# One activation table set for Ln and Exp, a reordered first norm, two tiles per block of h, and early weights in a two-layer hybrid decoder

## The chip, the cores and the metric

The kernel runs on one core of one Trainium2 chip. The metric is device time in microseconds (us), the median of several executions. All arithmetic is in 32-bit floats. Large products are made of three TensorE products of halves ("hi" and "lo" parts in the fp32r type), so that a product of two fp32 tiles costs three matmuls.

## The reference

Two layers, each an RMS norm, one input projection, three causal mixers that read the same normalised input, SiLU gates, one output projection and a residual add; one RMS norm after the last layer. The sequence is 1024 long, the model 1024 wide.

```python
def hybrid_layer(x, ...):
    h = rmsnorm(x, norm_gain)
    proj = h @ w_in
    (gq, gk, gv, gb, ga, gz, mq, mkv, mkr, mz, lx, lz) = jnp.split(proj, offsets, axis=-1)
    ...
    o_a = gated_delta_rule(q, k, v, g, beta)          # 4 heads of 128, chunks of 64
    o_a = rmsnorm(o_a, gdn_out_norm).reshape(B, S, GDN_WIDTH).astype(dt) * jax.nn.silu(gz)
    ...
    o_b = causal_block_attention(qf, kf, vm) * jax.nn.silu(mz)   # 8 heads, latent q and kv
    ...
    o_c = rg_lru(u, ...) * jax.nn.silu(lz)            # 512 channels, scan over the sequence
    mixed = jnp.concatenate([o_a, o_b, o_c], axis=-1)
    return x + mixed @ w_out

def rmsnorm(x, gain):
    y = x * lax.rsqrt(jnp.mean(x * x, axis=-1, keepdims=True) + RMS_EPS)
    return y * gain
```

## The kernel before

Activations lie transposed: 128 channels on the partitions, the 1024 positions along the free axis, in two halves of 512 (`n` = 0, 1). The normalised input `h` is eight blocks of 128 channels, each as a hi tile (`self.hh[k]`) and a lo tile (`self.hl[k]`). An output tile of the input projection is 128 channels; there are 38 of them per layer (`w_in`), each 2 halves x 8 blocks x 3 matmuls = 48 matmuls of 512 columns into one PSUM tile `pbig` of two banks. Two `pbig` tiles exist at a time.

**The order of the work** is a planner's. The program is traced in Python order, each instruction with a priority that grows with the trace; `self.prio(-LOW)` makes an instruction urgent, `self.prio(LOW)` makes it filler. The planner lays the instructions out on each engine by a model of their durations, and each engine then runs its own list strictly in order, waiting on semaphores. The load of an activation table is put in by a pass that comes after: ahead of an activation whose function isn't in the set that is loaded, it loads the first set that has it. Exp, Tanh, Square and Copy are in the set loaded first; Ln is in another. DMAs are all issued by SP's queue, also in order.

A layer has two stages. `phase_a` makes the input projection and runs the GDN and LRU mixers (`gates`, `gdn_tok`, `gdn_pre`, `gdn_inverse`, `gdn_prep`, `gdn_scan`, `gdn_norm`, `lat_q`, `lat_kv`, `lru`), with input-projection tiles as filler between the parts of the GDN chain. `phase_c` makes the latent attention, one head after the other, its softmax with Exp, and adds the output projection in pieces (`out_proj`, `out_proj_last`).

**The weights** of a projection tile are loaded by `load_w` (line 97): a DMA into `wst`, a cast to `whi` on VectorE (on ScalarE for narrow ones), and the remainder `wlo` on GpSimd. The pool `pw` has two of each, so a third tile's `whi` and `wlo` can be made only after the first tile's products have been done.

**The norm.** `rms_bcast` (line 180) adds up squares over the channels with matmuls against ones, then r = exp(-0.5 ln(mean + eps)) on ScalarE: an Ln, then an Exp. Line 186 is an Ln of one column that brings the table load ahead of the real Ln. `norm_half` (line 201) makes h block by block: `hf` = x * gain * r on VectorE, the hi cast on ScalarE, the lo remainder on VectorE, or with `share` on GpSimd for every other block. `first_norm` (line 924) does this for both halves of the input in turn; at the end of layer 0 it is done from `out_proj_last` (line 848), at the end of layer 1 the final norm writes the output.

**The first two tiles.** `gates` calls `in_tile(l, MT_MISC, MT_K)`: both tiles of a half are traced one after the other, MISC over all eight blocks of h, then K over all eight. The gates' inputs are copied out of MISC (line 219) and transposed (line 224).

**Memory.** Pools are laid out on a stack in the order of the `with` lines of `build` (line 878). `pw` of the next layer (2 x (wst + whi + wlo) of 4 KB per partition, 24 KB) starts where phase_c's first pool starts. That is `pp` (line 917): the softmax tiles P, four of 2 KB and four of 4 KB, 24 KB, in which `out_proj_last` also keeps its weights `wl`. After it lie `px` (four xt tiles, 8 KB), `pw` of phase_c (12 KB), and `pc` with the tiles k (eight of 2 KB), q, qr, v, o and others. A tile that is put where another was waits for that one's readers.

Of the kernel before, what the change touches and what calls it, by code (L numbers as in the profile page):

```python
# [16 lines left out]
DM = 1024  # L17
L = 2
H2 = 512
# [44 lines left out]
class Trunk:  # L64
# [20 lines left out]
    def act(self, out, in_, func, **kw):  # L85
        self.nc.scalar.activation(out, in_, func, **kw)  # L86
# [10 lines left out]
    def load_w(self, src, nk, cols, eng=None, pool=None):  # L97
# [6 lines left out]
        nc.sync.dma_start(st[:, :n], src.rearrange("p k c -> p (k c)"))  # L104
        hi = pool.tile([128, wn], F32R, name="whi", tag="whi")
        lo = pool.tile([128, wn], F32R, name="wlo", tag="wlo")
        with self.prio(-self.LOW):
            if wn <= 512:
                nc.scalar.copy(hi[:, :n], st[:, :n])  # L109
            else:  # L110
                nc.vector.tensor_copy(hi[:, :n], st[:, :n])  # L111
            (eng or nc.gpsimd).tensor_tensor(lo[:, :n], st[:, :n], hi[:, :n].bitcast(F32), ALU.subtract)  # L112
# [3 lines left out]
    def mm3(self, out, pairs):  # L116

        nc = self.nc
        n = len(pairs)
        for j, (ah, al, bh, bl) in enumerate(pairs):  # L120
            nc.tensor.matmul(out, ah, bh, start=(j == 0), stop=False)  # L121
            nc.tensor.matmul(out, ah, bl, start=False, stop=False)  # L122
            nc.tensor.matmul(out, al, bh, start=False, stop=(j == n - 1))  # L123
# [7 lines left out]
    def in_tile(self, l, *ms):  # L131

        if ms[0] not in self.ready:
            tiles = []
            for m in ms:
                hi, lo = self.early.pop(m, None) or self.load_w(self.i["w_in"][l, m], 8, 128)
                self.ready[m] = self.big()
                tiles.append((hi, lo, self.ready[m]))
            with self.prio(self.LOW):
                for n in range(2):  # L140
                    s = slice(n * H2, (n + 1) * H2)
                    for hi, lo, p in tiles:
                        self.mm3(p[:, s], [(hi[:, k], lo[:, k], self.hh[k][:, s], self.hl[k][:, s]) for k in range(8)])
        return self.ready.pop(ms[0])
# [26 lines left out]
    def add_squares(self, alloc, acc, x, eng):  # L171

        sq = alloc("sq")
        self.act(sq, x, AF.Square)
        if acc is None:
            return sq
        eng.tensor_tensor(acc, acc, sq, ALU.add)
        return acc

    def rms_bcast(self, alloc, accs, n, ch, tag, fine=False):  # L180
# [3 lines left out]
        if not fine:  # L184

            self.act(self.dummy, accs[-1][:, 0:1], AF.Ln, bias=self.eps)
        for s0 in range(0, n, H2):
            s = slice(s0, s0 + H2)
            pz = self.bank(tag)
            for j, a in enumerate(accs):  # L190
                nc.tensor.matmul(pz, self.one.to_broadcast([128, 128]), a[:, s],
                                 start=(j == 0), stop=(j == len(accs) - 1))
# [8 lines left out]
    def norm_half(self, alloc, xs, accs, n, gain, tag, share=False):  # L201

        r = self.rms_bcast(alloc, accs, H2, DM, tag)
        s = slice(n * H2, (n + 1) * H2)
        for k in range(8):
# [9 lines left out]
    def gates(self, l):  # L215
# [3 lines left out]
        nc.scalar.copy(misc, p)  # L219
# [92 lines left out]
    def gdn_tok(self, pr, P):  # L312
# [3 lines left out]
        for q in range(4):  # L316
            for src, dst in (("kT", "ktok"), ("vT", "vtok")):
# [6 lines left out]
                if src == "kT":  # L324
                    j = pa.tile([128, 128], F32, name="junk", tag="junk", bufs=1)
                    for c, u, hd, cs in self.combos(q):
                        self.act(j, kt[:, cs], AF.Square, accum_out=sk[:, q * 4 + c : q * 4 + c + 1])
# [3 lines left out]
        self.act(rk, sk, AF.Ln, bias=self.eps4)  # L331
# [8 lines left out]
        self.act(rq, P["sq"].rearrange("p t h -> p (t h)"), AF.Ln, bias=self.eps4)  # L340
# [146 lines left out]
    def gdn_norm(self, pr, P):  # L487
# [4 lines left out]
        for q in range(4):  # L492
            for c, u, hd, cs in self.combos(q):
                self.act(jk, P["attn"][q][:, cs], AF.Square, accum_out=ms[:, 4 * q + c : 4 * q + c + 1])
        self.tt(ms, ms, P["rq2"], ALU.mult)
        self.act(ms, ms, AF.Ln, scale=1.0 / 128.0, bias=self.eps)
# [101 lines left out]
    def lat_q(self, l):  # L598
# [16 lines left out]
        self.act(sq, ms, AF.Ln)  # L615
# [66 lines left out]
    def halves(self, tag, bufs):  # L682
        return [self.pc.tile([128, H2], F32R, name=tag, tag=tag, bufs=bufs) for _ in range(2)]
# [164 lines left out]
    def out_proj_last(self, wsrc, ops, xin, xout, alloc):  # L848
# [12 lines left out]
        for n in range(2):  # L861
            xs, accs = [], []
            for m in range(8):
                xt = self.pc.tile([128, H2], F32, name="xk", tag=("q", "qr")[n] if m < 6 else "k", bufs=6 if m < 6 else 8)
# [13 lines left out]
    def build(self):  # L878
# [5 lines left out]
        with sb("pk") as pk, sb("pg") as self.pg, sb("pf", 2) as self.pf, sb("ph", 16) as self.ph, \  # L884
# [19 lines left out]
            for l in range(L):  # L904
# [12 lines left out]
                with sb(f"pp{l}") as self.pp, sb(f"px{l}c", self.NX) as self.px, sb(f"pw{l}c", 2) as self.pw, \  # L917
# [6 lines left out]
    def first_norm(self, p0):  # L924
# [12 lines left out]
        al = lambda name: p0.tile([128, H2], F32, name=name, tag=name, bufs=8)  # L937
        for n in range(2):
# [4 lines left out]
            self.norm_half(al, xs[n], sq, n, self.par[:, C_NG : C_NG + 8], "st", True)  # L943
# [75 lines left out]
    def phase_c(self, l, xd):  # L1019
# [55 lines left out]
        else:  # L1075
            for n, xs, accs in self.out_proj_last(i["w_o2"][l, 3], ops[6:8], xd[3], None, al):
                s = slice(n * H2, (n + 1) * H2)
                r = self.rms_bcast(al, accs, H2, DM, "po")
# [111 lines left out]
```

## Time and profile before

| | |
|---|---|
| time, median of 3 runs | 2166.27 us (2162.41 to 2166.75) |
| the profiled execution | 2164.75 us, span 2163.0 us |
| mean granted TensorE clock | 0.989 |
| instructions | 28800 |
| busy, of the span: PE, PEld, DVE, ACT, POOL | 95%, 78%, 61%, 41%, 34% |
| HBM traffic | 102 GB/s over the span |

PE is TensorE's matmuls, PEld its weight loads, DVE VectorE, ACT ScalarE, POOL GpSimd, SP the engine that issues the DMAs; L123 is line 123 of the kernel. The columns of a row of the timeline are the start, the duration, engine, line, operation, out<-in, shapes, the number of instructions merged, and in brackets the idle time of the engine before it and what ended that. A row of the waits gives the engine and tile that waited, for whom, the total in us, how often, and the longest. A row of the windows gives the stretch, its length, and each engine's busy time with its number of instructions, then the granted clock, the share of the DMA engines and GB/s. A matmul is shown with its whole latency; matmuls overlap, so that the pace is the distance from one start to the next.

### The profile page before, as it was taken

To read this page: it belongs to the slowest core of one execution; us is meant where nothing else is said; L and a number is where in the kernel's file an instruction comes from. 1 tells how busy PE (TensorE), PEld (TensorE's weight loads), DVE (VectorE), ACT (ScalarE), POOL (GpSimd) and SP (SyncE) were. 2 spreads that over 40 slices of the span, in tenths; PEclk is the share of its full clock that TensorE was granted. 3 is DMA by queue.
4 is the path that set the end of the run, shared out by engine and by line. 5 is a ranking of instruction groups with operands and counts; after the bars stand their busy time and mean duration, and the time that the engine had idled before them with its cause. 6 is when DMAs were issued, how large, how long until landed. Compare 5 with 4: busy or idle time off the path is not lost. (4 is left out here: it accounts for less than half of the span.)

```text
span 2163.0 us, 28800 instructions
## 1 busy us (share of the span) xinstructions
PE 2055.8 (95%) x10380; PEld 1682.4 (78%) x10380; DVE 1320.9 (61%) x2498; ACT 883.2 (41%) x1790; POOL 729.9 (34%) x784
## 2 busy tenths in 40 slices
PE   7999999999989999999899999999998999999997
PEld 4888877787768788888668888787876877888874
DVE  6647556555851777776664575484468237676766
ACT  5241244135720554553542313522375125444535
POOL 3222333234451333332242323333336323233322
PEclk9999999999999999999999999999999999999999
DMA  4223212323253115335421321134223520335172
GB/s 142 87 78 101 70 59 93 99 77 103 67 171 128 43 38 186 103 124 175 153 91 39 113 83 54 59 103 132 71 67 113 175 96 28 114 109 179 53 233 97
DMA packets 135103, 222.08 MB, mean 103 GB/s; under 512 B 37808, under 2 KB 60336, under 8 KB 134960
## 3 DMA queue, kind: packets, MB, share of 16 engines
q1 hardware_dynamic: 134960, 220.24, 31.3%
q8 instruction: 82, 1.34, 0.3%
q14 instruction: 61, 0.50, 0.1%
HBM read 147.31 MB, written 72.88 MB: 102 GB/s over the span
## 5 line engine op out<-in xcount | busy, mean ns | idle before, releaser
L112 POOL TENSOR_TENSOR wlo<-wst,whi 128x1024 fp32r<-128x1024 f32 (+3 forms) x196 | 315.9, 1612 | 831.7 <-DVE whi L111 278.3
L121 PE MATMUL pbig<-h,whi 128*128 128x512 f32 x1216 | 483.9, 398 | 9.1 <-ACT h L127 6.1
L123 PE MATMUL pbig<-h,wlo 128*128 128x512 f32 x1216 | 484.4, 398 | 4.0 <-POOL wlo L112 4.0
L122 PE MATMUL pbig<-h,whi 128*128 128x512 f32 x1216 | 483.7, 398 | 2.9 <-POOL h L128 1.6
L121 PEld LDWEIGHTS pbig<-h,whi 128*128 128x128 f32 x1216 | 231.0, 190 | 54.9 <-ACT h L127 6.9
L122 PEld LDWEIGHTS pbig<-h,whi 128*128 128x128 f32 x1216 | 230.4, 190 | 50.4 <-DVE h L128 3.7
L123 PEld LDWEIGHTS pbig<-h,wlo 128*128 128x128 f32 x1216 | 230.6, 190 | 48.8 <-POOL wlo L112 5.3
L86 ACT ACTIVATE P<-pS,mx,scq 128x512 f32<-128x512 f32 (+1 forms) x192 | 128.0, 670 | 153.4 <-DVE mx L770 78.0
L111 DVE CAST whi<-wst 128x1024 fp32r<-128x1024 f32 x92 | 78.2, 850 | 138.2 <-PE pbig L122 105.2
L95 POOL TENSOR_SCALAR P<-P,mx 128x128 f32<-128x128 f32 (+6 forms) x112 | 79.8, 714 | 209.1 <-DVE mx L778 109.9
L109 ACT CAST whi<-wst 128x256 fp32r<-128x256 f32 (+2 forms) x104 | 46.5, 448 | 203.3 <-DMA wst<-in_w_uk 98.8
L127 ACT CAST pth<-pstp 128x512 fp32r<-128x512 f32 x192 | 90.8, 478 | 76.2 <-PE pstp L807 74.7
L767 DVE TENSOR_REDUCE mx<-pS 128x1 f32<-128x512 f32 (+1 forms) x192 | 106.6, 555 | 16.6 <-PE pS L761 10.4
L128 DVE TENSOR_TENSOR ptl<-pstp,pth 128x512 fp32r<-128x512 f32 x192 | 104.9, 552 | 16.0 <-ACT pth L127 15.6
L86 ACT ACT_TABLE_LOAD x81 | 103.9, 1283 | 14.6 <-DVE kT L89 11.9
L807 PE MATMUL pstp<-con,P 128*128 128x128 f32 x576 | 98.0, 275 | 6.1 <-DVE P L782 5.3
L92 DVE TENSOR_TENSOR xt<-pspj,xt 128x512 f32<-128x512 f32 x96 | 66.2, 690 | 50.4 <-PE pspj L123 24.3
L807 PEld LDWEIGHTS pstp<-con,P 128*128 128x128 f32 x576 | 71.9, 141 | 25.2 <-DVE P L782 7.1
L121 PE MATMUL pspj<-lh,whi 128*128 128x512 f32 x208 | 84.0, 404 | 2.6 <-DVE q L128 2.5
L818 PE MATMUL pspo<-pth,vh 128*128 128x512 f32 x192 | 79.5, 414 | 4.7 <-ACT pth L127 4.7
L122 PE MATMUL pspj<-ll,whi 128*128 128x512 f32 x208 | 81.8, 393 | 0.0
L123 PE MATMUL pspj<-lh,wlo 128*128 128x512 f32 x208 | 81.5, 392 | 0.0
(270 smaller groups left out, 4564.7 us busy)
## 6 DMA issues: line engine op xcount, KB each, us to landing
wst<-in_w_in SPq DMA_DIRECT2D x76, 512.0 KB, 3.6
x<-xt SPq DMA_DIRECT2D x128, 256.0 KB, 3.5
xt<-x SPq DMA_DIRECT2D x112, 256.0 KB, 3.6
mzd<-z SPq DMA_DIRECT2D x16, 512.0 KB, 3.5
wst<-in_w_o SPq DMA_DIRECT2D x16, 512.0 KB, 3.5
mz<-mzd SPq DMA_DIRECT2D x32, 256.0 KB, 3.0
wst<-in_w_o SPq DMA_DIRECT2D x64, 128.0 KB, 2.1
xk<-x SPq DMA_DIRECT2D x32, 256.0 KB, 4.3
```

Source lines behind the costliest of these rows:

```text
L86: self.nc.scalar.activation(out, in_, func, **kw)
L95: self.nc.gpsimd.tensor_scalar(out, a, s, 1.0, ALU.mult, ALU.mult)
L111: nc.vector.tensor_copy(hi[:, :n], st[:, :n])
L112: (eng or nc.gpsimd).tensor_tensor(lo[:, :n], st[:, :n], hi[:, :n].bitcast(F32), ALU.subtract)
L121: nc.tensor.matmul(out, ah, bh, start=(j == 0), stop=False)
L122: nc.tensor.matmul(out, ah, bl, start=False, stop=False)
L123: nc.tensor.matmul(out, al, bh, start=False, stop=(j == n - 1))
L127: self.nc.scalar.copy(hi, x)
L128: (eng or self.nc.vector).tensor_tensor(lo, x, hi.bitcast(F32), ALU.subtract)
L767: nc.vector.tensor_reduce(mx[:, j : j + 1], S[j], AX.X, ALU.max, negate=True)
L807: nc.tensor.transpose(tp[:, qi * 128 : qi * 128 + 128], P[qi][:, kb * 128 : kb * 128 + 128], self.ident)
L818: nc.tensor.matmul(po[:, w], vh[:, vs], th[:, w], start=(j == 0), stop=False)
```

## The change

- `ln_exp_set(prev)` loads the table set that holds both Ln and Exp, right behind the instruction `prev` on ScalarE; `behind` ties an instruction to another by an order that needs no semaphore. In `rms_bcast` it replaces the Ln of one column, for the first half of a norm only. In `gdn_tok` it stands behind the last square, and both Lns of that function behind it; also in `gdn_norm` and `lat_q`.
- `first_norm` makes the sums of the second half after four of the first half's eight blocks, and no longer gives every other lo remainder to GpSimd.
- `in_tile` goes over the blocks of h outside and over its tiles inside.
- For a call with two tiles the DMAs of the weights get the urgent priority (`soon`).
- The k tiles of attention get a pool of their own, `pkk`, the first of phase_c, followed by `px`; `pp` comes after them. So the next layer's `pw` lies on the k tiles (8 x 2 KB) and px (4 x 2 KB) instead of on P and `wl`. In `out_proj_last` the residual tiles of m = 6, 7 move out of the k tiles into `ob`.
- The copy of MISC out of PSUM is made in two halves.

```diff
+    def ln_exp_set(self, prev):
+        return self.behind(self.nc.scalar.preload_act_table_set("natural_log_exp_and_others"), prev)
...
-        nc.sync.dma_start(st[:, :n], src.rearrange("p k c -> p (k c)"))
+        with self.prio(-self.LOW if soon else 0):
+            nc.sync.dma_start(st[:, :n], src.rearrange("p k c -> p (k c)"))
...
-                hi, lo = self.early.pop(m, None) or self.load_w(self.i["w_in"][l, m], 8, 128)
+                hi, lo = self.early.pop(m, None) or self.load_w(self.i["w_in"][l, m], 8, 128, soon=len(ms) > 1)
...
-                    for hi, lo, p in tiles:
-                        self.mm3(p[:, s], [(hi[:, k], lo[:, k], self.hh[k][:, s], self.hl[k][:, s]) for k in range(8)])
+                    for k in range(8):
+                        for hi, lo, p in tiles:
+                            self.mm3(p[:, s], [(hi[:, k], lo[:, k], self.hh[k][:, s], self.hl[k][:, s])], k == 0, k == 7)
...
-        if not fine:
-            self.act(self.dummy, accs[-1][:, 0:1], AF.Ln, bias=self.eps)
+        table = table and self.ln_exp_set(self.last_square)
...
-            self.act(r[:, s], pz, AF.Ln, scale=1.0 / ch, bias=self.eps)
+            ln = self.act(r[:, s], pz, AF.Ln, scale=1.0 / ch, bias=self.eps)
+            if table:
+                self.behind(ln, table)
...
-        r = self.rms_bcast(alloc, accs, H2, DM, tag)
+        r = self.rms_bcast(alloc, accs, H2, DM, tag, table=n == 0)
...
-        self.act(rk, sk, AF.Ln, bias=self.eps4)
+        table = self.ln_exp_set(last)
+        self.behind(self.act(rk, sk, AF.Ln, bias=self.eps4), table)
...
-        self.act(rq, P["sq"].rearrange("p t h -> p (t h)"), AF.Ln, bias=self.eps4)
+        self.behind(self.act(rq, P["sq"].rearrange("p t h -> p (t h)"), AF.Ln, bias=self.eps4), table)
...
-        self.act(sq, ms, AF.Ln)
+        table = self.ln_exp_set(self.act(self.dummy, ms[:, 0:1], AF.Copy))
+        self.behind(self.act(sq, ms, AF.Ln), table)
...
-                with sb(f"pp{l}") as self.pp, sb(f"px{l}c", self.NX) as self.px, sb(f"pw{l}c", 2) as self.pw, \
+                with sb(f"pkk{l}") as self.pkk, sb(f"px{l}c", self.NX) as self.px, sb(f"pp{l}") as self.pp, sb(f"pw{l}c", 2) as self.pw, \
...
-            self.norm_half(al, xs[n], sq, n, self.par[:, C_NG : C_NG + 8], "st", True)
+            rs.append(self.rms_bcast(al, sq, H2, DM, "st", table=n == 0))
+            for j, ks in ((0, range(4)),) if n == 0 else ((0, range(4, 8)), (1, range(8))):
+                self.norm_apply(al, xs[j], rs[j], j, self.par[:, C_NG : C_NG + 8], ks)
```

More of the change, by code (lines that the diff above doesn't have):

```diff
@@ L85, in act, with behind @@
     def act(self, out, in_, func, **kw):
-        self.nc.scalar.activation(out, in_, func, **kw)
+        return self.nc.scalar.activation(out, in_, func, **kw)
+    def behind(self, ins, prev):
+        info = mybir.DependencyInfo(mybir.DependencyClass.NoSync, mybir.DependencyReason.DATA)
+        self.tc.add_manual_dep(ins.ins, prev.ins.name, info, reason="order on one engine")
+        return ins
+    def ln_exp_set(self, prev):
+        return self.behind(self.nc.scalar.preload_act_table_set("natural_log_exp_and_others"), prev)
     def stt(self, out, in0, s, in1, op0, op1):
@@ L114, in load_w, with mm3 @@
                 lo[:, :n].rearrange("p (k c) -> p k c", k=nk))
-    def mm3(self, out, pairs):
+    def mm3(self, out, pairs, start=True, stop=True):
         nc = self.nc
@@ L120, in mm3 @@
         for j, (ah, al, bh, bl) in enumerate(pairs):
-            nc.tensor.matmul(out, ah, bh, start=(j == 0), stop=False)
+            nc.tensor.matmul(out, ah, bh, start=(start and j == 0), stop=False)
             nc.tensor.matmul(out, ah, bl, start=False, stop=False)
-            nc.tensor.matmul(out, al, bh, start=False, stop=(j == n - 1))
+            nc.tensor.matmul(out, al, bh, start=False, stop=(stop and j == n - 1))
     def split(self, hi, lo, x, eng=None):
@@ L201, in norm_half, with norm_apply @@
     def norm_half(self, alloc, xs, accs, n, gain, tag, share=False):
-        r = self.rms_bcast(alloc, accs, H2, DM, tag)
+        r = self.rms_bcast(alloc, accs, H2, DM, tag, table=n == 0)
+        self.norm_apply(alloc, xs, r, n, gain, range(8), share)
+    def norm_apply(self, alloc, xs, r, n, gain, ks, share=False):
         s = slice(n * H2, (n + 1) * H2)
-        for k in range(8):
+        for k in ks:
             h = alloc("hf")
@@ L218, in gates @@
         misc = self.c4("misc")
-        nc.scalar.copy(misc, p)
+        for n in range(2):
+            nc.scalar.copy(misc[:, n * H2 : (n + 1) * H2], p[:, n * H2 : (n + 1) * H2])
         nc.sync.dma_start(self.krd, misc[0:64])
@@ L682, in halves @@
     def halves(self, tag, bufs):
-        return [self.pc.tile([128, H2], F32R, name=tag, tag=tag, bufs=bufs) for _ in range(2)]
+        return [(self.pkk if tag == "k" else self.pc).tile([128, H2], F32R, name=tag, tag=tag, bufs=bufs) for _ in range(2)]
     def attn_q_rope(self, l, pr, res):
@@ L863, in out_proj_last @@
             for m in range(8):
-                xt = self.pc.tile([128, H2], F32, name="xk", tag=("q", "qr")[n] if m < 6 else "k", bufs=6 if m < 6 else 8)
+                if m < 6:
+                    xt = self.pc.tile([128, H2], F32, name="xk", tag=("q", "qr")[n], bufs=6)
+                elif m == 6:
+                    both = self.pc.tile([128, 2, H2], F32, name="xk", tag="ob", bufs=6)
+                    xt = both[:, 0]
+                else:
+                    xt = both[:, 1]
                 self.out_tile(*W[m], ops, n, "pj", xt, xin[m], xout and xout[m])
@@ L937, in first_norm @@
         al = lambda name: p0.tile([128, H2], F32, name=name, tag=name, bufs=8)
+        rs = []
         for n in range(2):
@@ L1077, in phase_c @@
                 s = slice(n * H2, (n + 1) * H2)
-                r = self.rms_bcast(al, accs, H2, DM, "po")
+                r = self.rms_bcast(al, accs, H2, DM, "po", table=n == 0)
                 for k in range(8):
```

12 lines of the change are left out of this document (6 added, 6 removed).

## The prediction

> **What bounds the kernel now.** First the page's shares, then the windows view: the start, the first layer, the boundary between the layers, and a stretch of products alone.
>
> ```profile
> PE 2055.8 (95%) x10380; PEld 1682.4 (78%) x10380; DVE 1320.9 (61%) x2498; ACT 883.2 (41%) x1790; POOL 729.9 (34%) x784
> 0.00:56.00 56.00, 40.06 (x124) 23.63 (x125) 36.24 (x45) 33.31 (x59) 21.37 (x22) 0.91 0.42 145
> 56.00:1026.00 970.00, 939.53 (x4842) 780.05 (x4841) 588.22 (x1133) 382.44 (x781) 328.75 (x361) 0.99 0.31 100
> 1026.00:1118.00 92.00, 81.32 (x341) 59.42 (x341) 62.01 (x105) 48.58 (x100) 33.71 (x27) 0.96 0.40 134
> 1230.00:1260.00 30.00, 30.00 (x134) 24.86 (x133) 20.73 (x48) 2.86 (x3) 4.83 (x2) 1.00 0.34 106
> ```
>
> TensorE bounds it: inside the layer it is busy 97% of the time (939.53 of 970), and in 1230:1260, where it only multiplies, 134 products of 512 columns take 30 us, 0.224 us each. It is not the bound at the start (40 of 56) and at the layer boundary (81 of 92). The change takes no product away, so it can win only TensorE's waits. These are listed by the waits view of TensorE:
>
> ```profile
> PE pspr L367 <- DVE a L89: 5.7, 4, 2.2
> PE pspr L320 <- ACT ktok L322: 4.7, 4, 1.2
> PE pbig L123 <- POOL wlo L112: 4.0, 3, 2.7
> PE pspj L121 <- DVE xk L92: 3.3, 4, 1.3
> PE pspj L121 <- DVE q L128: 2.5, 2, 1.4
> PE pbig L121 <- DVE whi L111: 1.7, 1, 1.7
> L86 ACT ACT_TABLE_LOAD x81 | 103.9, 1283 | 14.6 <-DVE kT L89 11.9
> ```
>
> Each of these rows meets a part of the change. The 81 table loads of 1.28 us matter only where one of the waits stands behind them: ScalarE as a whole is busy 41%.
>
> **The first norm.** The timeline of the start:
>
> ```profile
> 12.28 2.43 DVE L111 CAST whi<-wst 128x1024 fp32r<-128x1024 f32 x1 [0.54 <-DMA wst<-in_w_in]
> 18.38 1.22 PE L121 MATMUL pbig<-h,whi 128*128 128x512 f32 x2 [6.07 <-ACT h L127]
> 20.68 0.63 PE L121 MATMUL pbig<-h,whi 128*128 128x512 f32 x1
> 21.11 0.63 PE L122 MATMUL pbig<-h,whi 128*128 128x512 f32 x1
> 24.09 0.63 PE L123 MATMUL pbig<-h,wlo 128*128 128x512 f32 x1
> 27.14 1.28 DVE L177 TENSOR_TENSOR sq<-sq 128x512 f32<-128x512 f32 x2
> 27.87 1.98 PE L191 MATMUL psst<-sq,ep 128*128 128x512 f32 x4 [0.39 <-DVE sq L177]
> 35.44 2.08 DVE L89 SCALAR_TENSOR_TENSOR hf<-x,par,rb 128x512 f32<-128x512 f32 x3 [4.15 <-ACT rb L86]
> 37.43 0.68 DVE L128 TENSOR_TENSOR h<-hf,h 128x512 fp32r<-128x512 f32 x1
> 38.03 1.77 DVE L89 SCALAR_TENSOR_TENSOR hf<-x,par,rb 128x512 f32<-128x512 f32 x1
> 46.44 1.28 POOL L128 TENSOR_TENSOR h<-hf,h 128x512 fp32r<-128x512 f32 x1 [1.28 <-ACT h L127]
> 49.60 0.44 PE L224 MATMUL pspr<-con,misc 128*128 128x128 f32 x2
> 50.04 2.38 POOL L112 TENSOR_TENSOR wlo<-wst,whi 128x1024 fp32r<-128x1024 f32 x1 [0.78 <-PE pspr L224]
> 55.31 0.39 PE L121 MATMUL pbig<-h,whi 128*128 128x512 f32 x1
> ```
>
> The 96 products of MISC and K start at 18.38, and the third tile starts at 55.31: 36.9 us, where 96 x 0.224 are 21.5. Until about 24.5 a product takes 0.43 (20.68 to 21.11), the half clock. Then the second half's blocks of h are missing: VectorE stands 4.15 us for r, and the last block comes at 46.44 + 1.28 = 47.7. Since MISC goes over all eight blocks alone, TensorE spends 3 products (0.67 us) per block and waits for the next.
>
> After: 6 products per block, 1.34 us. VectorE's price of a block is one hf (2.08 / 3 = 0.69) and one lo remainder (0.68 at 37.43), which overlap a little: about 1.3 us, without GpSimd, and supply and demand meet. The sums of the second half (four additions of 0.64, two at 27.14) stand inside this, so the 4.15 us go. VectorE begins at 14.7 at the earliest, since it makes whi until then (12.28 + 2.43), so an Exp that comes earlier helps little; 16 blocks and the sums take 14.7 + 21 + 2.6 + 2.4 for a remainder of GpSimd's like that at 50.04, beside which VectorE stands (the 1.77 at 38.03 is an hf beside GpSimd) = 41. TensorE is then the limit: start 18.4; 14 products at half clock 6.0; 82 x 0.224 = 18.4; sums 4.0 (two groups like that at 27.87): 46.8. New is a **wait behind the pair**: both tiles end together, and the third tile's remainder on GpSimd (2.38, the row at 50.04) can start only then, where until now it lay beside 24 products of K. I count 2.5, with the transposes inside (four pairs of 0.44 less overlap, the first at 49.60, about 1.3): third tile at 49.3. **Gain 6.0**; bounds 0 (blocks come at the slow pace still) and 9 (the remainder hidden).
>
> The clock gate bears on that new wait. [...] If it strikes, it costs 7 x 0.2 = 1.4 us at each place, which I keep in the range.
>
> **The layer boundary.**
>
> ```profile
> 1084.27 0.38 SPq L104 DMA_DIRECT2D wst<-in_w_in  x1
> 1089.02 0.68 ACT L86 ACTIVATE rb<-pspo,ep 128x512 f32<-128x512 f32 x1
> 1089.84 0.50 PE L121 MATMUL pbig<-h,whi 128*128 128x512 f32 x1 [1.69 <-DVE whi L111]
> 1093.27 0.79 PE L123 MATMUL pbig<-h,wlo 128*128 128x512 f32 x1 [2.71 <-POOL wlo L112]
> 1095.56 0.63 PE L122 MATMUL pbig<-h,whi 128*128 128x512 f32 x1
> L757 PE MATMUL pS<-k,q x96: 218/388/582, 709.7 to 1045.2; 128*128 128x512 f32 x48, 128*128 128x128 f32 x16, 128*128 128x256 f32 x16, 128*128 128x384 f32 x16
> ```
>
> The next layer's weights are requested at 1084.27, when the last products from `wl` are done. With the k tiles at that place they can come from about 1046, after the last scores (L757, the view of that line between 700 and 1100), and TensorE loses neither 1.69 nor 2.71, nor what the half clock costs from 1093.27 to 1095.56 (7 products x 0.2 = 1.4): 5.8. Against it: K's second bank is the one that holds the norm's sums until the Ln at 1089.02 has read them, which K now needs three products after the start instead of 24 (1.0), and the wait behind the pair, 2.5 less the 1.3 of transposes that now lie in it (1.2). **Gain 3.6**; bounds 0 and 7. SP's two requests, two casts of 0.7 on VectorE and two remainders of 2.4 on GpSimd move into the end of attention, where GpSimd is busy 33.71 of 92 us (1026:1118); if a remainder delays a softmax tile, TensorE waits for up to 2.4.
>
> **One table set.** Where an Exp stood 1.28 behind its Ln, it now follows at once. The end of the chain of waits, stretches of the timeline, and a row of the waits:
>
> ```profile
> 2132.88 1.28 ACT L86
> 2134.18 0.64 ACT rb L86
> 2150.59 1.28 ACT L86
> 333.50 1.28 ACT L86 ACT_TABLE_LOAD   x1
> 336.80 1.16 PE L367 MATMUL pspr<-kT 128*128 128x128 f32 x8 [2.20 <-DVE a L89]
> 126.22 1.28 ACT L86 ACT_TABLE_LOAD   x1
> 128.55 0.66 PE L320 MATMUL pspr<-con,kT 128*128 128x128 f32 x4 [1.24 <-ACT ktok L322]
> ACT z L86 <- PE pbig L123: 133.7, 19, 11.7
> ```
>
> At both norms behind `out_proj_last` the additions xk queue on VectorE behind the hf that waits for r, and TensorE behind xk: the 1.3 of the row "DVE xk", twice: **2.6**. The last half's Exp stands in the chain that ends the kernel, behind the load of 2150.59: **1.3**. [...]
>
> In `gdn_tok` four loads stand amid the copies for which TensorE's transposes wait (rq at 123 and 126, rk's pair later); after it is one before the Lns, and rq's two move behind the last square, where only `gdn_norm` needs them. Covered by this are the first two rows of the waits, 4.7 and 5.7. The planner lays the list out anew, and a wait that comes from its model being wrong need not go: of 10.4 I take **7.0** (bounds 2 and 10.4). Added are loads back to the set with Tanh, one after each of these places. A load runs before its Tanh's wait, and such Tanhs wait for products (133.7 us in total for z), so they are hidden; uncovered, eight of them cost 10.
>
> **The start of attention.** Its first weights now lie where LRU weights and operands of the first output blocks were, which are free earlier than before; the row "DVE q" (2.5, a cast that queues behind a late weight DMA) can go: **1.5**, bounds -2 and 5.
>
> **Sum.** 6.0 + 3.6 + 2.6 + 1.3 + 7.0 + 1.5 = 22.0. The span 2163.0 becomes 2141.0; the profiled execution has 1.75 around it, 2142.8, and the median of the runs is 1.5 above that execution: **2144 us**.
>
> **The rivals.**
>
> *The set isn't taken (8%).* If the pass still puts its own loads before the Lns and Exps, the terms 2.6, 1.3 and 7.0 fall: 2155. Against it: a load is put in only where the function is missing.
>
> *The first norm stays short of blocks (8%).* VectorE's hf takes 1.8 us instead of 0.7 while GpSimd works; for it speaks the 1.77 at 38.03, against it that GpSimd, busy there with a remainder, no longer makes any. Term 6.0 becomes 0: 2150.
>
> *The planner gives it back (18%).* Every duration it plans with changes from the start on; GDN's waits reappear elsewhere, and the loads back to Tanh strike a few times (7 + 1.5 lost, 3 added): 2156, with a tail to no gain.
>
> *More than the rows (11%).* Four terms come out near their high bounds, since waits behind those removed go too and the remainder behind the pair is hidden (9, 7, 10.4 and 2.5 for 6.0, 3.6, 7.0 and 1.5): 11 more, 2133.
>
> *SP's queue blocks (5%), the slow side.* The urgent request for the next layer's weights stands in one in-order queue with the xt, mz and w_o loads. A request that is placed when one head's k tiles are free and the next head's are not makes all of them wait.
>
> The scores (L757, 709.7 to 1045.2) take 335.5 us for eight heads, 42 each. Blocked for a whole head, SP delays the projection's operands by up to 42, at this one boundary: 2144 + 42 = 2186. It decides the sign from 22 us on. Against it: the planner places a request when its model has the place free, and in that model k's last reader comes then.
>
> **Chances and range.** The forecast has 50%, its own range 2138 to 2150. With the first two rivals, the one above and most of the planner's, 2132 to 2160 holds 8 in 10; the bounds of the terms (0 + 0 + 2.6 + 1.3 + 2 - 2 = 4 at the low end, 9 + 7 + 2.6 + 1.3 + 10.4 + 5 = 35 at the high end) reach 2162 and 2131. A measurement tells 0.2%, 4.3 us, from no change. Slower: SP's queue and a little of the planner's, 0.06; within: the tail of the planner's and of the low bounds, 0.07; faster 0.87.
>
> **What would show it.** Right: some 15 to 25 fewer table loads and none between Ln and Exp; VectorE without its 4.15 us wait; third tile at about 49; the request for layer 1's weights near 1046 and MISC's first product less than 1 us behind the sums; a wait of about 2.5 for wlo behind each pair; waits "DVE xk", "ACT ktok" and "DVE a" gone. Wrong: new TensorE waits within 56:1026, rows of Tanh behind a load that a product waits for, SP idle before a weight request with xt late.

## The result, and the profile after

The change makes the kernel faster: 2149.62 us, median of four runs (2147.64 to 2151.88), beside 2165.09 us for the kernel before on the same chip; the ratio is 0.9924, 95% interval 0.9911 to 0.9936. On another chip the same kernel gave 2146.36 and 0.9911 (0.9896 to 0.9926). One execution of that run (4102.59) and one of u5 below (3360.34) were far slower than all others and are left out of the medians. The prediction was 2144, with 2132 to 2160 as its range: the sign and the range held, the likeliest time was 5.6 us too low. The profiled execution has a span of 2145.7, so 17.3 us less than before, where the sum of the prediction had 22.0.

The kernel after: the engines' busy time from its page, and from the view of its lines the two groups of table loads (L96 is the line of the new load, L86 what the pass still puts in).

```profile
PE 2050.1 (96%) x10380; PEld 1681.6 (78%) x10380; DVE 1302.2 (61%) x2506; ACT 858.0 (40%) x1771; POOL 719.8 (34%) x776
L86 ACT ACT_TABLE_LOAD x49 | 62.9, 1283 | 17.9 <-DVE y L99 15.2 <-PE pbig L134 1.2 <-PEq L1213 0.7
L96 ACT ACT_TABLE_LOAD x15 | 19.2, 1283 | 0.2
```

There are 64 table loads instead of 81. TensorE multiplies as long as before (2050.1 and 2055.8 us) in a shorter span. What it waits for, in the waits view of the kernel after:

```profile
PE pspr L525 <- POOL at L105: 6.2, 4, 1.7
PE pspo L840 <- DVE ptl L139: 6.1, 10, 2.1
PE pbig L134 <- POOL wlo L123: 4.5, 4, 1.6
PE pbig L132 <- ACT rb L86: 0.9, 1, 0.9
PE pspj L132 <- DVE xk L102: 0.6, 2, 0.3
PE pspr L338 <- ACT ktok L340: 0.3, 1, 0.3
```

The waits for a (5.7) and for ktok (4.7) are gone or nearly so, and that for xk went from 3.3 to 0.6. The wait for wlo has its 4.0 back as 4.5. Two of those that grew matter below: ptl, at the end of a head's attention, 3.6 before and 6.1 now with one of 2.1; and at, the transposes of `gdn_norm` behind GpSimd, which the waits of before don't have.

Where the span went is seen by cutting it at events that both kernels have. The starts are those of TensorE's rows in the timeline: the first product of the third tile, the first transpose of `gdn_tok`, the last product of the input projection, the first and the last score, the first matmul of the norm's sums at the end of layer 0, the first product of layer 1. Of the last product and of the scores it is the first of the group of matmuls that make one. Each number is the distance from the event ahead of it, in us; the columns after the first two are runs of the next section.

```
                                    before   after  r_after      u3      c1      b1      v2
A  start to third tile, layer 0      55.31   48.17    47.83   47.39   46.51   48.60   47.62
B  to gdn_tok                        67.67   70.67    70.65   67.68   70.67   67.68   67.68
C  to last product of projection    473.00  468.79   469.47  469.44  469.76  467.76  470.20
D  to first score                   113.69  112.01   112.49  112.80  113.18  112.19  112.65
E  to last score                    335.50  335.40   333.88  337.33  332.55  334.56  335.09
F  to sums of the norm               20.90   24.96    25.06   24.25   21.30   21.30   20.89
G  to first product, layer 1         23.77   20.27    20.26   20.24   20.25   20.23   22.50
H  to third tile, layer 1            27.86   24.04    24.04   23.53   24.04   23.53   28.90
I  to gdn_tok                        67.68   71.92    70.60   67.65   71.95   67.65   67.67
J  to last product of projection    472.01  468.64   467.67  471.06  468.02  470.99  469.26
K  to first score                   112.76  112.50   112.23  112.91  112.79  113.23  112.73
L  to last score                    336.64  335.26   334.53  335.54  332.75  335.20  335.58
M  to the end of the span            56.18   53.03    54.45   53.01   53.04   53.05   53.63
```

After against before: A wins 7.1, and B loses 3.0 of it. C and J, the two GDN stages, win 4.2 and 3.4. G and H at the layer boundary win 3.5 and 3.8 as meant, but F ahead of them and I behind them lose 4.1 and 4.2, so the boundary as a whole (F to I) is 141.2 where it was 140.2. M wins 3.2.

The loss in F, from the timeline of the kernel after at the end of layer 0's attention:

```profile
1036.22 0.86 SPq L115 DMA_DIRECT2D wst<-in_w_in  x2
1041.41 0.69 DVE L122 CAST whi<-wst 128x1024 fp32r<-128x1024 f32 x1
1042.55 2.37 POOL L123 TENSOR_TENSOR wlo<-wst,whi 128x1024 fp32r<-128x1024 f32 x1
1042.61 2.86 DVE L122 CAST whi<-wst 128x1024 fp32r<-128x1024 f32 x1
1045.40 0.68 DVE L139 TENSOR_TENSOR ptl<-pstp,pth 128x512 fp32r<-128x512 f32 x1
1046.13 0.80 PE L840 MATMUL pspo<-ptl,vh 128*128 128x512 f32 x1 [2.08 <-DVE ptl L139]
1048.01 0.63 PE L839 MATMUL pspo<-pth,vl 128*128 128x512 f32 x1
```

The request for layer 1's weights is early, at 1036.22 (before: 1084.27). The first cast takes 0.69. The second starts 0.06 us behind GpSimd's remainder and takes 2.86; the softmax remainder ptl stands behind it on VectorE, TensorE waits 2.08, and its next products take 0.8 and 0.63 instead of 0.4: the half clock (granted 0.52 from 1046 to 1049.4).

The loss in I, the third tile of layer 1:

```profile
1103.44 0.39 PE L134 MATMUL pbig<-h,wlo 128*128 128x512 f32 x1
1103.83 0.44 PE L242 MATMUL pspr<-con,misc 128*128 128x128 f32 x2
1103.88 4.99 POOL L123 TENSOR_TENSOR wlo<-wst,whi 128x1024 fp32r<-128x1024 f32 x2 [7.30 <-PE pbig L134]
1104.31 0.50 PE L132 MATMUL pbig<-h,whi 128*128 128x512 f32 x1
1106.60 0.50 PE L134 MATMUL pbig<-h,wlo 128*128 128x512 f32 x1 [1.55 <-POOL wlo L123]
1107.77 0.77 PE L134 MATMUL pbig<-h,wlo 128*128 128x512 f32 x1
...
1109.48 0.77 PE L133 MATMUL pbig<-h,whi 128*128 128x512 f32 x1
```

The pair's last product starts at 1103.44; only then can the third tile's remainder be made. The third tile starts with its two products that need whi alone and waits 1.55 for wlo, and here the half clock follows (granted 0.54 from 1107.0 to 1110.5, 1.00 from 1103.0 to 1106.5). One pair of the transposes of MISC (L242) lies ahead of the wait; the other three stand behind the waiting product in TensorE's list and don't fill its wait. They are no more work than before: there all four pairs lie ahead of the third tile, in A and H, and now three of them lie in B and I (104 and 317 matmuls in H and I before, 98 and 323 after). In I that is 1.3 of the 4.2.

### The profile page after: what moved, and what is told of

Its sections match the earlier page's. It is cut to its first block, busy times and chain, and to the rows that moved or that the text cites. A ratio compares the mean times of both kernels' runs of the same rounds, so it can differ in the third digit from the quotient of the medians.

```text
span 2145.7 us, 28793 instructions
## 1 busy us (share of the span) xinstructions
PE 2050.1 (96%) x10380; PEld 1681.6 (78%) x10380; DVE 1302.2 (61%) x2506; ACT 858.0 (40%) x1771; POOL 719.8 (34%) x776
## 5 line engine op out<-in xcount | busy, mean ns | idle before, releaser
L86 ACT ACTIVATE P<-pS,mx,scq 128x512 f32<-128x512 f32 (+1 forms) x192 | 128.0, 669 | 155.6 <-DVE mx L790 78.9
L86 ACT ACTIVATE z<-pbig 128x1024 f32<-128x1024 f32 x24 | 24.6, 1026 | 146.2 <-PE pbig L134 143.0
```

What stands on the lines that cost most here:

```text
L86: return self.nc.scalar.activation(out, in_, func, **kw)
```

## The experiments

Twelve kernels, all timed against the kernel before. `u` undoes an edit of the kernel after, `c` and `b` add something to it, `v` adds edits to the kernel before.

| run | edit | median us | ratio to before, 95% |
|---|---|---|---|
| r_after | none | 2146.36 | 0.9911 (0.9896 to 0.9926) |
| u1_tables | table loads as before | 2157.21 | 0.9962 (0.9951 to 0.9973) |
| u2_first | first norm as before | 2147.30 | 0.9906 (0.9893 to 0.9918) |
| u3_blocks | tiles in turn as before | 2143.90 | 0.9891 (0.9878 to 0.9904) |
| u4_place | pools, xk, request as before | 2154.66 | 0.9944 (0.9932 to 0.9956) |
| u5_both | u2 and u3 | 2145.89 | 0.9910 (0.9894 to 0.9927) |
| c1_calm | casts, remainders behind attention | 2140.31 | 0.9878 (0.9862 to 0.9893) |
| c2_third | third tile's wlo on VectorE | 2145.83 | 0.9900 (0.9885 to 0.9914) |
| c4_lo_late | remainders alone behind attention | 2149.69 | 0.9918 (0.9904 to 0.9932) |
| b1_blocks_calm | u3 and c1 | 2139.49 | 0.9873 (0.9860 to 0.9887) |
| v1_tables_only | before, with the table set | 2157.99 | 0.9952 (0.9938 to 0.9966) |
| v2_no_place | v1, with the new first norm | 2148.15 | 0.9918 (0.9904 to 0.9931) |

An interval is some 3 us wide to each side, so a difference of 2 or 3 us between two of these totals says little; the stretches of the traces say more. The first run is for that comparison:

> The kernel after once more, for a comparison on one chip with the three beside it. All theories: 2149.6, between 2147 and 2152, and the same rows in its trace apart from the arrival of the first loads.

It came out at 2146.4, a little below that range, and its stretches differ from those of the kernel after by up to 1.5 us each (E 1.5, M 1.4, I 1.3), but by 0.1 at most in B, F, G and H.

**The table set.** Undone alone in the kernel after, and made alone in the kernel before:

```diff
     def ln_exp_set(self, prev):
-        return self.behind(self.nc.scalar.preload_act_table_set("natural_log_exp_and_others"), prev)
+        return None
...
```

In u1 `behind` also does nothing, and the Ln of one column is back in `rms_bcast`.

> The kernel after, with the Ln and Exp loads as in the kernel before and all else kept. The changed kernel's median is 2149.6. Theory (the gain in gdn_tok and at the three norm ends comes from the table set): the Exps behind each Ln wait 1.28 us again, the table loads return from 64 to about 81, the TensorE waits for ktok and a return, and the stretch from the third tile to the last scan of layer 0 loses its 1 to 3 us; with both layers 4, the two norms behind out_proj_last 2.6 and the last Exp 1.3 that makes 2149.6 + 7.9 = 2157.5, between 2154.5 and 2160. Rival (the planner's new list made the gain in gdn_tok, not the set): only the 3.9 of the norm ends go, 2153.5, and the waits for ktok and a stay away.

> The kernel before with the Ln and Exp edits alone (and MISC's copy in two halves): first norm, order of the tiles, pools, xk and weight request as before. Theory (the set is the largest part, some 8 of the 16, and does not need the others): 64 table loads, no wait for a, nearly none for ktok, 2159 (2156.5 to 2161). Rival (the gain in gdn_tok comes from what the other edits do to the list): 2163, the two norm ends alone.

Without the set the time is 2157.2, some 8 to 11 us above the kernel after (ratios 0.9962 against 0.9924 and 0.9911); with the set alone it is 0.9952 x 2167.3, so 10.4 below before. Both agree with the theory, not with the 4 us of the rival. Rows of u1's page and waits, one fence each:

```profile
L86 ACT ACT_TABLE_LOAD x81 | 103.9, 1283 | 2.1 <-PEq L1213 0.7
```

```profile
PE pspr L386 <- DVE a L97: 5.6, 4, 2.2
PE pspr L338 <- ACT ktok L340: 4.7, 4, 1.2
PE pspj L130 <- DVE q L137: 1.7, 2, 0.9
```

The 81 loads and both waits are back, to 0.1 us of their old size, and so is most of the wait for q (2.5 before). The transposes of `gdn_tok` show it at one place: first and last start of layer 0's first sixteen, of u1 and then of the kernel after (the view of that line).

```profile
L338 PE MATMUL pspr<-con,kT x16: 270/272/329, 118.5 to 128.6; 128*128 128x128 f32 x16
```

```profile
L338 PE MATMUL pspr<-con,kT x16: 272/273/328, 118.8 to 123.4; 128*128 128x128 f32 x16
```

Ten microseconds become under five. Not all of it lasts: the stretches C and J together are 945.0 before and 946.3 in u1, and between 936.9 and 944.2 (mean 939.5) in the twelve traces that have the set. So the set is worth about 6 in GDN, but a single pair of traces tells it badly: 8.8 from u1 to the kernel after, 3.8 from before to v1. One thing that takes from it is the new wait for at, 6.2 in all, which u1 doesn't have and v1 has. Leaving the set out of `gdn_norm` alone wasn't tried.

**The start: new order of the norm, or two tiles per block.**

```diff
-            rs.append(self.rms_bcast(al, sq, H2, DM, "st", table=n == 0))
-            for j, ks in ((0, range(4)),) if n == 0 else ((0, range(4, 8)), (1, range(8))):
-                self.norm_apply(al, xs[j], rs[j], j, self.par[:, C_NG : C_NG + 8], ks)
+            self.norm_half(al, xs[n], sq, n, self.par[:, C_NG : C_NG + 8], "st", True)
```

> The kernel after, with the first norm as before: each half's eight blocks in turn, the second half's sums behind all of the first half's, every second remainder on GpSimd; two tiles per block kept. Theory (the new order and VectorE alone bring the start): hf beside GpSimd takes 1.8 instead of 0.7 us again, VectorE's wait of about 4 us for r returns, the third tile of layer 0 starts at 53 to 55 instead of 48.2, and the time is 2149.6 + 5.5 = 2155 (2153 to 2157). Rival (two tiles per block alone suffice, since products then cover the supply): third tile by 50, 2149 to 2151.5.

```diff
-                    for k in range(8):
-                        for hi, lo, p in tiles:
+                    for hi, lo, p in tiles:
+                        for k in range(8):
                             self.mm3(p[:, s], ..., k == 0, k == 7)
```

> The kernel after, with MISC gone over for all eight blocks of a half before K, as before; all else kept. Theory (the supply of h, one block in about 1.3 us, sets the start, and the order of the tiles only says what waits at its end): K's second half, 24 products of 0.224 = 5.4, follows the last block at about 42.5, so the third tile starts at 48.5 to 50 instead of 48.2, but its wait of about 1.6 for wlo and the half clock behind it go at both layer starts, since MISC's weight buffers come free 5 us earlier: 2148 to 2151, no change that can be told. Rival (two tiles per block carry most of the gain at the start, as my forecast had it): third tile at 52 or later, 2153 to 2155.

> The kernel after with both edits of its first products undone: first norm as before, and MISC for all eight blocks of a half before K. Each undone alone left the third tile of layer 0 where it is (49.0 and 47.4). Theory (either of the two suffices: fewer blocks missing, or more products per block): without both VectorE waits some 4 us for r again and the third tile starts at 53 to 55; no wait for wlo at the third tile of either layer; against the run with the tiles in turn (2143.9) some 6 lost: 2150, between 2148 and 2152. Rival (the order of the norm alone is what counts, and the u2 run was lifted by two tiles per block only): the same. Second rival (neither counts, the start gains from the table set and the list): third tile by 50, 2142 to 2146.

Neither undo makes the kernel slower, and with the tiles in turn (u3) it is rather faster, below what I expected. A + B, from the start to `gdn_tok`, tells more than the third tile: 123.0 before, 121.2 in u5 (neither edit), 120.9 in u2 (two tiles per block alone), 115.1 in u3 (new order alone), 118.8 in the kernel after (both). The new order is worth 4.9 to 6.1 of this (121.2 to 115.1 in u3 and to 116.3 in b1, which has the same first products). Two tiles per block are worth 0.3 without it and cost 1 to 4 with it: the six traces with both (c2 below left aside) have 117.1 to 118.8, the three with the new order alone 115.1 to 116.3. For u2 the third tile comes at 49.0 instead of 53.5, but B grows from 67.6 to 71.9 and takes that back. The tile order moves the work; what starts early at the third tile is paid there. My u2 expectation was wrong (it said a third tile at 53 to 55 and 2155, and 49.0 and 2147.3 came, nearer to its rival): its third tile was early after all, and what it loses in A + B, 2.1, is within the interval of the totals. For u5 the third tile came as expected, at 53.5, and the time, 2145.9, 2 us below its range. The layer-1 part of the same order is H + I: 96.0 and 94.6 with it, 91.2 without (u3, and b1).

**The wait behind the pair.**

```diff
+            if third:
+                for j in range(2):
+                    c = slice(j * 512, (j + 1) * 512)
+                    nc.vector.tensor_tensor(lo[:, c], st[:, c], hi[:, c].bitcast(F32), ALU.subtract)
+            else:
+                (eng or nc.gpsimd).tensor_tensor(lo[:, :n], st[:, :n], ...)
```

> The kernel after, with the remainder of the third tile's weights (one tile per layer) made by VectorE in two halves of 0.7 instead of by GpSimd in one of 2.4. Theory (the wait behind the pair, and what the half clock adds behind it, is why the kernel with the tiles in turn is faster): the waits of 1.6 for wlo at 50.5 and 1106.6 fall under 0.6, no product of 0.4 us or more follows them, 2 x 2.4 = 4.8 less: 2145 (2143.5 to 2147). Rival (only the waits count, the half clock costs nothing): 2147. Second rival (tiles in turn are faster for what else the list does): 2149.6, no change.

Both waits are gone, and no product at the third tile takes over 0.5. B falls from 70.7 to 69.0 and I from 71.9 (in r_after 70.6) to 69.0. The 1.3 that stay above the 67.7 of the tiles in turn are the six transposes, which there lie ahead of the third tile: they have moved and cost nothing. So behind the pair two tiles per block cost 1.6 of wait, and at layer 1 of the kernel after 1.3 more, the half clock. With both gone, A + B is 115.6 in c2, as with the tiles in turn, but H + I is still 93.0 beside 91.2; 0.9 of that is a wait for r (rb) at K's second bank, which the tiles in turn don't have. The total, 2145.8, is 0.5 below r_after where the expectation had 4.8; the intervals can't tell the two apart. On the side this run shows VectorE slow beside GpSimd's remainder again (timeline of c2 at layer 0):

```profile
46.54 3.47 DVE L126 TENSOR_TENSOR wlo<-wst,whi 128x512 fp32r<-128x512 f32 x2
46.76 2.70 POOL L128 TENSOR_TENSOR wlo<-wst,whi 128x1024 fp32r<-128x1024 f32 x1 [17.63 <-PE pspr L247]
```

Two halves, each expected at 0.7 (the remainder of h, of the same 128x512, took 0.68 at 37.43 of before), take 3.47, to the end of GpSimd's remainder (46.76 + 2.70 = 49.46) and 0.55 more.

**The collision at the end of attention.** First the casts and remainders both behind it, then the remainders alone:

```diff
+            if soon:
+                self.behind(whi, self.last_ptl)
+                self.behind(wlo, self.last_ol)
```

> The kernel after, with one order added: the casts of the next layer's first two weights stand behind the last softmax remainder on VectorE, their remainders behind the last head's remainder on GpSimd. The request for the weights stays early. Theory (the early casts and remainders collide with the end of attention): the wait of 2.08 for ptl at 1046 and the half clock behind it go, the stretch from the last score to the norm's sums is 3 to 4 us shorter, MISC still finds its weights, and the time is 2146 (2144.5 to 2147.5). Rival (those 4 us are the order of the list, not the collision): the wait stays within 0.5 of what it was, or the weights come late; 2149 or more.

> The kernel after with only the two remainders of the next layer's first weights moved on GpSimd, behind the last head's remainder; their casts on VectorE stand where they stood, ahead of the softmax remainders. Theory (GpSimd's remainder slows VectorE's cast from 0.7 to 2.9, and that makes ptl late): both casts take 0.7, TensorE waits less than 0.8 for that ptl, no half clock follows, and the stretch from the last score to the norm's sums is 21.3 to 22.7 instead of 25.0: 2141 to 2143. Rival (two casts ahead of ptl in VectorE's queue are the delay): the wait stays 1.4 or more, the stretch 23.5 to 25, 2144.5 or more.

In c1 the casts run one behind the other at 1050.47, behind the last ptl, and TensorE has no wait for ptl there:

```profile
1040.46 1.29 DVE L142 TENSOR_TENSOR ptl<-pstp,pth 128x512 fp32r<-128x512 f32 x2 [0.32 <-ACT pth L141]
1041.29 0.42 PE L843 MATMUL pspo<-ptl,vh 128*128 128x512 f32 x1
1050.47 1.29 DVE L122 CAST whi<-wst 128x1024 fp32r<-128x1024 f32 x2
1055.26 4.69 POOL L123 TENSOR_TENSOR wlo<-wst,whi 128x1024 fp32r<-128x1024 f32 x2
```

F is 21.3 instead of 25.0, and G and H keep what they won (20.25 and 24.04): the weights are still in time. The 3.7 is what the theory said. The total fell by 6.0 against r_after, more than that; E and L account for 1.3 and 1.8 of it. In these two stretches TensorE's list is the same, instruction for instruction, in all the kernels here, so this part can't be put down to the edit.

In c4 the casts stand in VectorE's list where they stood, ahead of ptl, with GpSimd's remainders moved away:

```profile
1042.72 0.69 DVE L122 CAST whi<-wst 128x1024 fp32r<-128x1024 f32 x1
1043.92 0.68 DVE L122 CAST whi<-wst 128x1024 fp32r<-128x1024 f32 x1
1044.52 0.68 DVE L141 TENSOR_TENSOR ptl<-pstp,pth 128x512 fp32r<-128x512 f32 x1
1045.26 0.51 PE L842 MATMUL pspo<-ptl,vh 128*128 128x512 f32 x1
1054.25 0.41 ACT L140 CAST wl<-wst 128x256 fp32r<-128x256 f32 x1 [1.31 <-DMA wst<-in_w_o]
1055.69 0.33 PE L840 MATMUL pspo<-pth,vh 128*128 128x128 f32 x1 [1.15 <-ACT pth L140]
```

The second cast takes 0.68 instead of 2.86, ptl is in time, and TensorE doesn't wait for it. So it is GpSimd's remainder beside the cast, not the cast's place in the queue, that made ptl late. The total doesn't show it: F is 23.1, since a new wait of 1.15 stands at 1055.69, where ScalarE had waited 1.31 for a weight of the output projection ahead of pth, and 2149.7 is as much as the kernel after. My figure of 2141 to 2143 was wrong; what brings the rest of that total isn't settled.

**What the early weights are worth.**

```diff
-                with sb(f"pkk{l}") as self.pkk, sb(f"px{l}c", self.NX) as self.px, sb(f"pp{l}") as self.pp, ...
+                with sb(f"pp{l}") as self.pp, sb(f"px{l}c", self.NX) as self.px, ...
...
-                ... self.load_w(self.i["w_in"][l, m], 8, 128, soon=len(ms) > 1)
+                ... self.load_w(self.i["w_in"][l, m], 8, 128)
```

> The kernel after, with the pools, the xk and the weight request of the next layer as before; all else kept. Theory (the early weights won at the boundary, but their casts and remainders cost some 4 us at the end of attention): the request goes back to about 1075, TensorE waits again for whi and wlo of MISC (together some 4 us and a few us of half clock), but the wait of 2.08 for ptl at 1046 and the half clock behind it go; with the start of attention (1.5) the time is 2149.6 + 3 = 2152.5, between 2150.5 and 2154. Rival (the forecast's terms as they stood, no collision): 3.6 + 1.5 = 5.1, so 2154.7 or more. A second rival (the place brings nothing at the start of attention): 2151.

> The kernel before with the table edits and the new order of the first norm alone: MISC for all eight blocks of a half before K, pools, xk and weight request as before. It is b1 without the early weights. Theory (the early weights are worth their rows once the collision and the wait behind the pair are away): last score of layer 0 to the norm's sums 20.9, sums to the first product of layer 1 22.5, from there to the third tile 28, then 67.7, so 139 where b1 has 132.7; with about 1 for the start of attention 7 more than b1: ratio to before 0.990 to 0.9915, some 2147. Rival (the list gives the difference back, so early weights bring nothing): the ratio of b1, 0.9873, within its interval.

Undone in the kernel after, the time rises to 2154.7, 5 to 8 above it. That is the rival's time, not my theory's, though not for its reason: F is 20.9 as before, so the collision was there, and the waits for whi (1.7) and wlo come back. The waits view of u4 between 1030 and 1125:

```profile
PE pbig L134 <- POOL wlo L123: 4.7, 2, 3.1
PE pbig L132 <- DVE whi L122: 1.7, 1, 1.7
```

Only 1 to 2 us of the rise lie at the boundary: F to I is 142.0, beside 141.2 in the kernel after and 140.0 in r_after. C and J are 6.8 longer than in the kernel after, E and L 3.1; the edit doesn't explain that.

The cleaner comparison is v2 against b1, both with the tiles in turn: F to I is 140.0 without the early weights and 132.7 with them, and the ratios are 0.9918 and 0.9873, some 10 us of 2167. The expectation had 7, the rival none.

**Both losses taken away.**

> The kernel after with two edits: MISC for all eight blocks of a half before K again, and the casts and remainders of the next layer's first weights behind the last softmax remainder and the last head's remainder. Theory (both losses are separate: the collision at the end of attention, and the wait behind the pair with the transposes that it pushes into the third tile): from the last score of layer 0 to the norm's sums 21.3, from the first product of layer 1 to the third tile 23.5, from there to the first transposes of gdn_tok 67.7 in both layers; against the run with the calm order alone (2140.3) 4.5 less, 2136, between 2133 and 2138. Rival (what the tiles in turn win is given back in the later list, as one trace of that run showed 2.9 at layer 1's preparation): 2139 or more.

F, H and I are 21.30, 23.53 and 67.65, each as the theory had it, and G is 20.23. All that TensorE waits for at the boundary (waits view of b1 between 1030 and 1125):

```profile
PE pspj L136 <- POOL o L142: 0.8, 1, 0.8
PE pspj L135 <- DVE xk L102: 0.3, 1, 0.3
PE pS L780 <- ACT P L86: 0.3, 1, 0.3
PE pstp L830 <- POOL P L105: 0.2, 1, 0.2
```

The time is 2139.5, the best median here, 27.8 us below before (2167.28 on that chip), where the change itself has 15.5 and, on the other chip, 20.9. Against c1 it won 0.8 and not 4.5: F to I are 4.8 shorter than in c1, while E, J and L are 2.0, 3.0 and 2.5 longer. This was the rival's number, and its reason only in part, since the tile order doesn't change TensorE's list in E and L.

## Why the prediction came out as it did

Term by term, the stretches of the profiled executions beside the sum of 22.0; r_after is the same program once more:

```
term of the sum                        forecast   measured   r_after
first norm (A and B)                        6.0        4.1       4.5
layer boundary, with the xk there (F-I)     4.9       -1.0       0.3
gdn_tok (C and J)                           7.0        7.6       7.9
start of attention (D and K)                1.5        1.9       1.7
last norm: xk and last Exp (M)              2.6        3.2       1.7
not in the sum (E and L)                      -        1.5       3.7
sum                                        22.0       17.3      19.8
```

**The table set was right**, in mechanism, and in size as far as the totals tell it. The last norm's Ln and Exp follow each other, in the timeline of the kernel after:

```profile
2115.08 1.28 ACT L96 ACT_TABLE_LOAD   x1
...
2118.01 0.69 ACT L86 ACTIVATE rb<-pspo,ep 128x512 f32<-128x512 f32 x1 [1.64 <-PE pspo L203]
2118.73 0.63 ACT L86 ACTIVATE rb<-rb 128x512 f32<-128x512 f32 x1
```

The waits named are gone, and two runs from opposite sides give 8 to 11 us for terms of 10.9. The rival that the set isn't taken falls with the 15 loads of L96.

In one place the set was taken and lost: in layer 1's second `gdn_norm` a Tanh (z) was planned between the load and its Ln. `behind` fixes which comes first, and keeps nothing out from between them. ScalarE in the timeline of the kernel after:

```profile
1536.47 1.28 ACT L96 ACT_TABLE_LOAD   x1
1537.76 1.28 ACT L86 ACT_TABLE_LOAD   x1
1539.05 1.03 ACT L86 ACTIVATE z<-pbig 128x1024 f32<-128x1024 f32 x1
1540.09 1.28 ACT L86 ACT_TABLE_LOAD   x1
1541.39 0.31 ACT L86 ACTIVATE ms<-ms,ep 128x16 f32<-128x16 f32 x1
1541.71 1.28 ACT L86 ACT_TABLE_LOAD   x1
```

**The layer boundary is the step that failed.** The end of the norm in the timeline of the kernel after:

```profile
1076.37 4.46 PE L203 MATMUL pspo<-sq,ep 128*128 128x512 f32 x10
1080.27 0.80 PE L132 MATMUL pbig<-h,whi 128*128 128x512 f32 x1
```

What it was to win came: the request was early, MISC's first product starts as the sums end, K's second bank costs 0.9 where I had 1.0, and G and H together win 7.3, of which 1.3 are the transposes that now lie in I. Two costs were mis-sized; with 4.1 and 1.7 they make nearly all of the 5.9 by which the boundary fell short:

- The casts and remainders "move into the end of attention, where GpSimd is busy 33.71 of 92 us", and I put nothing for them into the sum. They cost 4.1. I looked at GpSimd's load, and for a remainder ahead of a softmax tile on GpSimd. What happened is a VectorE cast that runs 2.86 instead of 0.69 because GpSimd's remainder runs beside it; the first norm's rows had shown the same (hf 1.77 instead of 0.69 beside GpSimd), and I used it there alone. c4 shows it (0.68 without the remainder beside it), c1 the price (3.7 of it comes back).
- The wait behind the pair was 2.5 less 1.3 of transposes "that now lie in it". The wait is 1.55, but only one pair of transposes lies ahead of it; the others are queued behind the waiting product and fill nothing of it. With the half clock behind it (1.3, I 71.9 beside 70.6 in r_after) the place costs 2.9 at layer 1 of the kernel after and 1.6 in r_after, not 1.2.

Of TensorE's two waits at this boundary before the change, only one has the half clock behind it: the two products behind the wait of 1.69, at 1089.84 and 1090.17, take 0.50 and 0.39, and the granted clock is 0.97 from 1089.8 to 1093.2; behind the 2.71 it is 0.50 (1093.2 to 1095.6). That the half clock can strike behind the pair's wait, which the prediction kept in the range, was right: 0.54 behind the 1.55 at layer 1 of the kernel after.

**The first norm** has the same second error: A alone won 7.1, and B gave back 3.0, the wait of 1.6 and the 1.3 of transposes that the forecast had counted ahead of the third tile. It also had the wrong reason. "6 products per block" was to make supply and demand meet; u3 shows that the new order and VectorE alone do it, with three products per block, and better, because K's 24 products per half lie behind the last block and hide the third tile's weights. The rival "stays short of blocks" falls with it: A + B are 115.1 in u3.

**The start of attention** came out in size by luck, as far as the runs show. The forecast gave it to the weights' new place. But the wait for q is gone in u4, v1 and v2 too, where the weights lie as before, and 1.7 of it is back in u1, where they lie in the new place and the table set is out. D + K is 226.5 before, 225.4 in b1 with the new place and 225.4 in v2 without it.

**The rivals.** SP's queue didn't block: nothing near 42 us is missing between the scores and the norm. "The planner gives it back" has one clear instance, the wait for at. "More than the rows" (2133) did not come. The shortfall lies for the most part in the two costs above: in b1, with F and I at 21.3 and 67.65, the boundary wins 7.5 instead of losing 1.0.

## What to carry to other kernels

A load that is made earlier brings its casts and remainders with it: look for what they run beside, on every engine (here a cast of 0.69 took 2.86 beside a remainder), and order the helpers behind the critical work when only the transfer has to be early. When two tiles are interleaved so that they end together, whatever waited for the first one's buffers loses its cover; work that is to fill a wait must stand ahead of the waiting instruction in that engine's list (here three pairs of transposes stood behind it, and TensorE waited 1.55). Undo each edit alone and in pairs: here one of the edits was a loss inside a gain, and it only showed when it was taken out.

## What the runs showed of the hardware that I had not expected

A VectorE cast of 128x1024 that starts 0.06 us behind a GpSimd remainder ends 0.55 us behind that remainder's end (1042.61 + 2.86 against 1042.55 + 2.37); the same cast without it takes 0.68 (1043.92 of c4). c2's remainder on VectorE, with two inputs in SBUF, also ends 0.55 behind GpSimd's (46.54 + 3.47 against 46.76 + 2.70, and at layer 1 1101.33 + 3.47 against 1101.65 + 2.60). ptl, with one input in PSUM, took 0.68 at 1046.60 of the kernel after, although GpSimd made the second remainder from 1045.56 to 1047.93. What sets these cases apart no run here shows.

The same program met the half clock in one execution and not in another: behind the same wait of 1.55 at the third tile of layer 1, the windows view gives for 3.5 us in the kernel after and then in r_after (columns: stretch, length, busy time and instructions of PE, PEld, DVE, ACT, POOL, granted clock, DMA share, GB/s):

```profile
1107.00:1110.50 3.50, 3.50 (x14) 2.78 (x13) 1.35 (x3) 1.45 (x7) 1.88 (x1) 0.54 0.64 191
```

```profile
1106.50:1110.00 3.50, 3.50 (x18) 2.59 (x18) 2.16 (x3) 2.27 (x9) 1.76 (x1) 1.00 0.62 186
```

Seven of the traces here have this wait (1.55 to 1.62) at the third tile of both layers; the half clock followed it in 3 of these 14 places, at layer 1 in the kernel after and c1, at layer 0 in u2 (the stretch behind it, I or B, is 71.9 there, and 70.6 to 70.7 in the other four of the kernel after, r_after and c1).

And a stretch with the same list varies by more than one would think: E is 335.40 and 333.88 in two executions of one program, and from 332.4 to 337.3 over the kernels here. Two kernels that are to be compared within 3 us need their stretches compared, not only their totals.
